# Four VectorE sums of a gate operand moved into the first gate pair, three residual sums moved behind a weight split

## The chip, the cores and the metric

The kernel runs on one core of one Trainium2 chip. The metric is the device time of one execution in microseconds, taken as the median of several runs. The kernel is written with explicit tiles; a compiler pass puts the instructions of each engine in an order and adds the semaphores. Where the code asks for it, an instruction is kept in program order on its engine; elsewhere the pass may move it.

## The reference, cut to what matters

One layer of a diffusion backbone runs on 640 tokens (512 of a sample, 128 of a prompt) with a width of 1024. Four token mixers a, b, c and d each give a 256-wide result. Each is projected to 1024 and multiplied by a sigmoid gate, and the sum goes through `w_o` and is added to the residual:

```python
g_a, g_b, g_c, g_d = split(sigmoid(h @ w_gate + b_gate), 4)        # h: 640 x 1024
merged = (g_a * (y_a @ w_br_a) + g_b * (y_b @ w_br_b)
          + g_c * (y_c @ w_br_c) + g_d * (y_d @ w_br_d))             # y_*: 640 x 256
x = x + g1 * (merged @ w_o)
h = rmsnorm(x, norm2_g) * (1 + sc2) + sh2
x = x + g2 * conv_ffn(h, w_up, ...)
```

All of it is float32. The kernel keeps that accuracy by splitting each operand into a high and a low part and adding three products: high times high, high times low, low times high. The high part is a copy on ScalarE (ACT), the low part a subtraction on VectorE (DVE), so every weight block costs one instruction on each of the two engines before TensorE (PE) can use it.

## The kernel before, in words

**Order of the stages.** Boot and adaLN; the input projection with the four mixers run beside it as generators that a planner resumes; the gates; the output projection `w_o`; the second norm; the up projection of the FFN; the down projection. TensorE is the engine that most stages are ordered around.

**Gates.** The branches come in the order d, a, b, c. Of branch d, the output blocks n = 0 and n = 4 are made singly by `gate_tile` (the product of gate and branch is written to MG by a VectorE multiply, L1014). All others are made in pairs of blocks (n, n + 4) by `g_pair`, 15 pairs, with a Winograd form of a 2 x 2 block product: seven products (`GPROD`, numbered 1 to 7) instead of eight. Products 1 to 4 take blocks of the operand as they are, products 5, 6 and 7 take differences of them. The seven products with the 1024-deep h are called `gprod` (12 matmuls each, L1187), the seven with the 256-deep branch operand `bprod` (3 matmuls each, L1196).

**Operands of h.** The generator `g_operands` (L1036 on) loads quarters of h into D, G and S0, makes the differences there (L1052), splits them into F (product 7), X1 (product 5) and X0 (product 6), and makes one more operand in D for product 3 (L1070). Once the operand of product 7 is split, its place in D is free, and `y_load(0)` puts the operand of branch d there: SP copies the high part from E, and then POOL adds the low part with an accumulating DMA (both are `D<-E`). `y_sums` makes the differences of that operand in place: four VectorE instructions of 128x320, `D<-D`. They wait for the accumulating DMA. Then the flag `gx3` is set.

**The first pair.** `g_all` waits for that flag while it is being written out, and then makes the weights of pair 0: `g_s01` (s, two sums), `g_s23` (raw, two sums), `g_b` and `g_c` (the splits into w), `g_zh` (ACT, `S<-raw`). From there on the order of VectorE, ScalarE and POOL is fixed as written, until the last pair is done. `g_pair(0)` begins with `g_zl` (DVE, `S<-raw,S`) and product 1 into b1, whose copy by ACT is `ga<-m`; `g_a` (ACT, `B<-raw`) and, in a pair that begins a branch, `y_split` (ACT, two copies `C<-D`) follow; then product 2 into b3, `g_split(3)` (ACT `XH<-D`, DVE `XL<-D,XH`), the sum of b1 and b3 (DVE `ga<-m,ga`), the sums of pair 1's weights (DVE `D<-raw,G`, `D<-D,G`), the gate's sigmoid (ACT `ga<-ga,cst`), the low parts of `y_split` (DVE `C<-D,C`), product 6 and its copy (ACT `gb<-m`), product 5, and product 7. For the branches a, b and c, `y_sums` is called at the end of the pair before the one that needs it.

**Output projection.** `wo_tile` has eight units: two halves nh of the columns by four blocks kk of the depth. For nh = 0 the four blocks are accumulated into five PSUM tiles, one for each 128 tokens (t); behind the last block each is multiplied by the gain row (DVE, L1403, `wt<-m,F`) and added to the residual (DVE, L1405, `X<-X,wt`, and `G<-G,wt` for t = 4). For nh = 1 the products wait until all four weight blocks are there. Each weight block is split by ACT (L323) and DVE (L324, `w<-raw,w`). The tiles `wt` come from a pool of four buffers. Beside this, `up_early` prepares the first weights of the up projection on the same engines (L1525, L1544, L1548), and behind each finished t of nh = 1 `norm2(t)` starts: square on ACT (L1423), a root on POOL, the scaling on DVE (L1425), and eight transposes on TensorE (L1437).

Of the kernel before, what the change touches and what calls it, by code (L numbers as in the profile page):

```python
# [13 lines left out]
ALU = mybir.AluOpType  # L14
# [56 lines left out]
def tile_step(ctx: ExitStack, tc: tile.TileContext, a: dict, outs: list, dbg=None):  # L71
# [54 lines left out]
    def nm(s):  # L126
        cnt[0] += 1
        return f"{s}_{cnt[0]}"
# [26 lines left out]
    ten, vec, pool = [Ordered(e, boot) for e in (nc.tensor, nc.vector, nc.gpsimd)]  # L155
# [882 lines left out]
    def g_operands():  # L1038
        while "cg" not in R:
            yield 1  # L1040
        d, g = region("D", [P, 2, 4, HC]), region("G", [P, 4, HC])
        yield 8
        for x, h, c in ((d[:, 0], 0, 1), (d[:, 1], 1, 1), (g, 0, 0)):
            yield 10
            nc.sync.dma_start(x, hdr[h, c])
        while "scores" not in R or "ada39" not in R:
            yield 1
        a12 = region("S0", [P, 4, HC])
        nc.sync.dma_start(a12, hdr[1, 0])
        a21, a22, a11 = d[:, 0], d[:, 1], g  # L1050
        for o, x, y in ((a22, a21, a22), (a21, a11, a21), (a11, a22, a11)):
            tc.keep_in_program_order(vec.tensor_tensor(o, x, y, ALU.subtract))  # L1052
            yield 2
        gx["x"] = {}
        for i, h, c in ((1, 0, 0), (2, 1, 0), (4, 1, 1), (3, 0, 1)):
            cs = slice(c * HC, (c + 1) * HC)
            gx["x"][i] = xh[:, 4 * h:4 * h + 4, cs], xl[h][:, :, cs]
        for i, x, t, key in ((7, a21, "F", "scores"), (5, a22, "X1", "yc"), (6, a11, "X0", "yc")):
            while key not in R:
                yield 1  # L1060
            y = region(t, [P, 2, 4, HC], F32R)
            gx["x"][i] = y[:, 0], y[:, 1]
            g_split(i, x)
            if i == 7:
                gx["Y"] = a21.rearrange("p a t -> p (a t)")
                y_load(0)
            yield 1.5
        gx["t3"] = a22, a11
        gx["S"] = a22.rearrange("p a t -> p (a t)").rearrange("p (i k c) -> p i k c", i=2, k=5)
        vec.tensor_tensor(a22, a12, a11, ALU.add)  # L1070
        y_sums()
        R["gx3"] = True

    def g_split(i, x):
# [13 lines left out]
    def y_sums():  # L1088

        a11, a21, a12, a22 = [gx["Y"][:, i * HC:(i + 1) * HC] for i in range(4)]  # L1090
        for o, x, y, f in ((a22, a21, a22, ALU.subtract), (a21, a11, a21, ALU.subtract),
                           (a11, a22, a11, ALU.subtract), (a12, a12, a11, ALU.add)):
            ovec.tensor_tensor(o, x, y, f)
# [47 lines left out]
    def g_s01(p_, r):  # L1141

        s = gw[p_, "S"] = [gx["S"][:, i] if p_ else gp.tile([P, 5, P], F32, tag="gt", name=nm("s"))
                           for i in range(2)]
        ovec.tensor_tensor(s[0], r[0][:, 0], r[1][:, 1], ALU.add)
        ovec.tensor_tensor(s[1], s[0], r[1][:, 0], ALU.add)
# [90 lines left out]
    def g_pair(p_, r):  # L1237
        n, q = p_ + 1, p_ - 1
        inner, nx = p_ < GPAIR, n < GPAIR
        if not inner:  # L1240
            g_sig(q, 1, gw[q, "gt", 1], gw[q, "gt", 1])
            g_close(q)
            g_merges(q)
            return
        bi, n0 = gp_id(p_)
        new = n0 == (NPL if bi == 0 else 0)
        if new:
            gx["bi"] = bi
        if n0 == (NPL if bi == 0 else 0) + 1 and bi < 3:
            y_load(bi + 1)  # L1250
        b1, b3 = pm()[:, 0:HC], pm()[:, 0:HC]
        ga = gw[p_, "gt", 0] = gp.tile([P, T], F32, tag="gt", name=nm("ga"))
        gb = gw[p_, "gt", 1] = gp.tile([P, T], F32, tag="gt", name=nm("gb"))
        g_zl(p_, r[p_])
        gprod(b1, p_, 1, True)
        if q >= 0:
            g_sig(q, 1, gw[q, "gt", 1], gw[q, "gt", 1])
        oact(b3 if q >= 0 else ga[:, 0:HC], b1, AF.Copy)
        if q >= 0:
            g_close(q)  # L1260
        ps = gw[p_, "ps"] = pg()
        p1_, p3_ = ps[:, 1, 0:HC], ps[:, 0, 0:HC]
        bprod(p1_, p_, 1, True)
        oact(p3_, p1_, AF.Copy)
        if q >= 0:
            g_merges(q)
        if nx:
            g_a(n, r[n])
            if q >= 0:
                g_s01(n, r[n])  # L1270
        lows, x3 = y_split() if new else ([], None)
        gprod(b3, p_, 2, q < 0)
        if q < 0:
            g_split(3, gx["t3"][0])
            ovec.tensor_tensor(ga[:, 0:HC], b3, ga[:, 0:HC], ALU.add)
            g_s01(n, r[n])
        g_sig(p_, 0, ga[:, 0:HC], b3 if q >= 0 else ga[:, 0:HC])
        for x in lows:
            low(*x)
        if nx:  # L1280
            g_al(n, r[n])
            g_s23(n, r[n])
        gprod(b1, p_, 6, False)
        oact(gb[:, 0:HC], b1, AF.Copy)
        bprod(p3_, p_, 2, False)
        b2 = pm()[:, 0:HC]
        gprod(b2, p_, 5, True)
        if nx and not new:
            g_b(n)
        gprod(b1, p_, 7, False)  # L1290
        oact(gb[:, HC:T], b1, AF.Copy)
        y = gw[p_, "y"] = gp.tile([P, T], F32, tag="gt", name=nm("y"))
        c2_ = gw[p_, "b2"] = pm()[:, 0:HC]
        bprod(p1_, p_, 6, False)
        oact(y[:, 0:HC], p1_, AF.Copy)
        bprod(c2_, p_, 5, True)
        ovec.tensor_tensor(gb[:, HC:T], b2, gb[:, HC:T], ALU.subtract)
        if new:
            g_b(n)
        if nx:  # L1300
            late = g_c(n, r[n])
            if not new:
                for x in late:
                    low(*x)
            if n + 1 < GPAIR:
                r[n + 1] = gp_load(n + 1)
        else:
            m_split(0)
            m_split(1)
        gprod(b1, p_, 4, False)  # L1310
        g_sig(p_, 0, ga[:, HC:T], b1)
        bprod(p1_, p_, 7, False)
        oact(y[:, HC:T], p1_, AF.Copy)
        if new:
            oact(x3[2], x3[1], AF.Copy)
            low(*x3)
        if nx:
            g_zh(n, r[n])
        gprod(b2, p_, 3, False)
        if n0 == (NPL if bi == 0 else 0) + 1 and bi < 3:  # L1320
            y_sums()
        ovec.tensor_tensor(y[:, HC:T], c2_, y[:, HC:T], ALU.subtract)
        ovec.tensor_tensor(gb[:, 0:HC], b2, gb[:, 0:HC], ALU.subtract)
        if new:
            for x in late:
                low(*x)
# [40 lines left out]
    hh = []  # L1367
    st2 = const.tile([P, 16], F32, name="st2")

    wo = {}  # L1370

    def wo_tile(nh, kk_, w):
        if (nh, kk_) == (0, 0):
            start(up_early(), 1)
            drain(lambda: "ada39" in R)
            grows["g1"] = gain_load(0, "F")
            xr0 = region("X0", [P, 2560])
            xr1 = region("X1", [P, 2560])
            xr2 = region("G", [P, 1280])
            x2.extend([xr0[:, 0:1024], xr0[:, 1024:2048], xr1[:, 0:1024], xr1[:, 1024:2048],  # L1380
                       xr2[:, 0:1024]])
            for t in range(5):
                pool.dma_start(x2[t], xsrc[t])
            wo["acc"] = [pm(), pm(), pg()[:, 0, :], pm(), pg()[:, 0, :]]
        wo[kk_] = w
        if nh == 1 and kk_ < 3:
            return
        for t in range(5):
            m = pm() if nh == 1 else wo["acc"][t]
            for q in (range(4) if nh == 1 else (kk_,)):  # L1390
                for k in (2 * q, 2 * q + 1):
                    for i, (hx, hw) in enumerate(((0, 0), (0, 1), (1, 0))):
                        mm(m, mh[MHN[q]][:, hx, k % 2, t * P:(t + 1) * P], wo[q][:, hw, k % 2, :],  # L1393
                           start=(k == 0 and i == 0), stop=(k == 7 and i == 2))
                    tick(0.65)
            if (nh, kk_, t) == (0, 3, 4):
                R["half"] = True
            if kk_ < 3:
                continue
            v = 0 if t < 4 else 1  # L1400
            tmp = gp.tile([P, 512], F32, tag="gt", name=nm("wt"))
            cs = slice(nh * 512, nh * 512 + 512)
            vec.tensor_tensor(tmp, m, grows["g1"][:, v, cs], ALU.mult)  # L1403
            xs = x2[t][:, cs]
            vec.tensor_tensor(xs, xs, tmp, ALU.add)  # L1405
            if nh == 1:
                start(norm2(t))
                tick(0)
# [52 lines left out]
    for nh in range(2):  # L1461
        for kk_ in range(4):
            plain(lambda nh=nh, kk_=kk_: rows(a["w_o"][nh, MHN[kk_]], 2, 512,
                                              "MG0" if (nh, kk_) == (1, 0) else None),
                  lambda w, nh=nh, kk_=kk_: wo_tile(nh, kk_, w))
# [1099 lines left out]
```

## Time and profile before

| what | value |
|---|---|
| median of 3 runs (lowest, highest) | 1006.76 us (1006.0, 1009.12) |
| the profiled execution's own time | 1006.04 us |
| its span, first to last instruction | 1004.2 us |
| mean granted TensorE clock | 0.995 |
| busy: PE / DVE / ACT / POOL | 98% / 87% / 58% / 17% |
| chain that ended last: PE / DVE / DMA | 88% / 5% / 4% |

The busy shares are means over stages with different limits. A busy PE in these views is modelled, since matmuls are pipelined; what counts for it is where it had to wait and for whom. Names left of `<-` are what an instruction writes, those on the right what it reads; `L151` is the line of the helper through which the ordered instructions go, so in the gates an instruction is known by its tiles.

### The profile page before, as it was taken

How to read it: one execution, taken by the hardware profiler on the slowest of the kernel's cores; microseconds unless marked ns; L12 is line 12 of the kernel's file. 1: busy time of each engine (PE TensorE's matmuls, PEld its weight loads, DVE VectorE, ACT ScalarE, POOL GpSimd, SP SyncE). 2: the span in 40 equal slices, each digit the busy share in tenths (PEclk: the TensorE clock that was granted, in tenths of full speed). 3: DMA queues.
4: the chain of work that ended last, by engine and by line, in shares of the span. 5: the costliest groups of instructions: out<-in, count | busy, mean ns of one | idle time of the engine just before them, and what ended most of it. 6: DMA issues, size and time to landing. Idle time of an engine off the chain costs nothing.

```text
span 1004.2 us, 18954 instructions
## 1 busy us (share of the span) xinstructions
PE 987.3 (98%) x7452; PEld 935.0 (93%) x7452; DVE 869.5 (87%) x1425; ACT 587.2 (58%) x1018; POOL 168.3 (17%) x225
## 2 busy tenths in 40 slices
PE   8999999999989999999999999999999999999997
PEld 6899999999989999999998799999999999888886
DVE  6678899878769889898878978999999998999796
ACT  6642343445446555655656377777777777756672
POOL 1000020322111223241000021222222222100004
PEclk9999999999999999999999999999999999999999
DMA  9875344498465799899248875766666666976842
GB/s 353 334 252 163 111 149 124 125 258 252 120 215 179 275 230 287 248 276 235 85 132 331 321 284 181 219 159 174 173 163 169 177 169 194 353 259 226 292 127 105
DMA packets 70730, 212.86 MB, mean 212 GB/s; under 512 B 9713, under 2 KB 24849, under 8 KB 67953
## 3 DMA queue, kind: packets, MB, share of 16 engines
q1 hardware_dynamic: 43968, 151.22, 43.0%
q0 software_dynamic: 26672, 60.43, 26.3%
q8 instruction: 58, 0.95, 0.4%
q14 instruction: 32, 0.25, 0.1%
HBM read 168.62 MB, written 48.51 MB: 216 GB/s over the span
## 4 chain that ended last, share of the span: by engine, by line
PE 88%; DVE 5%; DMA 4%; issue 1%; POOL 1%; ACT 1%; SPq 0%; POOLq 0%; DVEq 0%; ACTq 0%
PE g L1623 21%; PE m L1187 18%; PE g L375 12%; PE m L2095 9%; PE m L1623 5%; PE g L2095 4%; PE g L1196 3%; PE g L948 2%; PE m L1393 2%; PE m L151 2%; PE g L151 1%; PE m L1196 1%; DMA D<-E 1%; PE m L539 1%; PE m L1618 1%
## 5 line engine op out<-in xcount | busy, mean ns | idle before, releaser
L375 PE MATMUL g<-XH,w 128*128 128x320 f32 x640 | 155.0, 317 | 0.0
L375 PEld LDWEIGHTS g<-XH,w 128*128 128x128 f32 x640 | 109.5, 188 | 2.5 <-issue 1.2
L375 PE MATMUL g<-XL,w 128*128 128x320 f32 x320 | 98.8, 309 | 0.0
L1187 PE MATMUL m<-XH,w 128*128 128x320 f32 x368 | 87.4, 309 | 0.0
L1187 PEld LDWEIGHTS m<-XH,w 128*128 128x128 f32 x368 | 63.2, 188 | 0.2 <-ACT gb L151 0.2
L375 PEld LDWEIGHTS g<-XL,w 128*128 128x128 f32 x320 | 60.3, 188 | 0.0
L2095 PE MATMUL m<-w,XH 128*128 128x512 f32 x246 | 58.6, 390 | 0.0
L1187 PE MATMUL m<-XL,w 128*128 128x320 f32 x184 | 56.9, 309 | 0.0
L2095 PEld LDWEIGHTS m<-w,XH 128*128 128x128 f32 x246 | 46.1, 188 | 9.5
L151 ACT ACTIVATE w<-raw 128x640 fp32r<-128x640 f32 (+3 forms) x54 | 49.8, 938 | 3.4 <-DMA raw<-in_w_in_dram 2.0
L1187 PE MATMUL m<-X,w 128*128 128x320 f32 x264 | 45.2, 320 | 3.7 <-ACT ga L151 3.7
L151 DVE TENSOR_TENSOR w<-raw,w 128x640 fp32r<-128x640 f32 (+3 forms) x46 | 46.9, 1037 | 0.9 <-ACT w L151 0.8
L1187 PEld LDWEIGHTS m<-X,w 128*128 128x128 f32 x264 | 41.8, 197 | 4.0 <-ACT ga L151 4.0
L151 POOL DMA_DIRECT2D wsum<-in_w_dn_dram x36 | 37.8, 1407 | 32.1 <-issue 26.4
L151 DVE SCALAR_TENSOR_TENSOR X<-MG,p2t,X 128x641 f32<-128x641 f32 x44 | 38.9, 883 | 1.0 <-ACT X L151 0.2
L151 DVE SCALAR_TENSOR_TENSOR X<-X,p2t,X 128x641 f32<-128x641 f32 x44 | 38.9, 883 | 0.9
L1623 PE MATMUL g<-XL,w 128*128 128x320 f32 x240 | 38.6, 310 | 0.0
L151 ACT ACTIVATE gb<-m 128x320 f32<-128x320 f32 x30 | 13.1, 437 | 43.5 <-PE m L1187 43.5
L1623 PE MATMUL g<-XL,C 128*128 128x320 f32 x240 | 38.3, 309 | 0.0
L1623 PEld LDWEIGHTS g<-XL,w 128*128 128x128 f32 x240 | 36.0, 188 | 0.6 <-ACT MG L151 0.3
L1623 PEld LDWEIGHTS g<-XL,C 128*128 128x128 f32 x240 | 35.9, 188 | 0.0
L1187 PEld LDWEIGHTS m<-XL,w 128*128 128x128 f32 x184 | 34.5, 188 | 0.0
(614 smaller groups left out, 2869.4 us busy)
## 6 DMA issues: line engine op xcount, KB each, us to landing
wsum<-in_w_dn_dram POOLq DMA_DIRECT2D x30, 512.0 KB, 11.9
raw<-in_w_up_dram SPq DMA_DIRECT2D x30, 512.0 KB, 5.2
raw<-in_w_gp_dram SPq DMA_DIRECT2D x23, 640.0 KB, 6.6
raw<-in_w_in_dram SPq DMA_DIRECT2D x19, 512.0 KB, 4.3
H<-in_w_adt_dram SPq DMA_DIRECT2D x19, 512.0 KB, 3.8
raw<-wsum SPq DMA_DIRECT2D x12, 512.0 KB, 5.8
actx<-X POOLq DMA_DIRECT2D x22, 256.0 KB, 5.0
wsum<-wsum POOLq DMA_DIRECT2D x10, 512.0 KB, 12.6
```

What stands on the lines that cost most here:

```text
L151: r = f(*args, **kw)
L375: mm(o, w[:, h, k0 + k, :], r(k)[:, s], start=(k == 0 and i == 0), stop=(k == kt - 1 and i == 2))
L539: mm(m[W * g:W * g + W, (i - s0) * W:(i - s0 + 1) * W], lhs, rhs, start=True, stop=True, tile_position=(64 * par, W * g))
L948: mm(o, x(kx)[:, ts], w[:, h, k, :], start=(kx == 0 and i == 0), stop=(kx == 7 and i == 2))
L1187: mm(o, w[:, h, n, k, :], x[:, k, :], start=(first and k == 0 and j == 0), stop=(k == 3 and j == 2), skip_group_check=True)
L1196: mm(o, w[:, h, n, 4, :], x[l], start=(first and j == 0), stop=(j == 2), skip_group_check=True)
L1393: mm(m, mh[MHN[q]][:, hx, k % 2, t * P:(t + 1) * P], wo[q][:, hw, k % 2, :], start=(k == 0 and i == 0), stop=(k == 7 and i == 2))
L1618: mm(o, w[:, k, :], x[:, k, :], start=(first and not part and k == 0 and j == 0), stop=(part == 1 and k == 3), skip_group_check=True)
L1623: z = mm(o, w[:, k, :], x[:, k, :], start=(first and k == 0 and j == 0), stop=(k == 3 and j == 2), skip_group_check=True)
L2095: mm(ps, s[t // 4][:, hx, k, o:o + P], w[:, hw, k, c0:c1], start=first, stop=i == 2 and bi == len(batch) - 1 and k == len(ks) - 1, skip_gr ...
```

## The change

`y_sums` for branch d is no longer called in `g_operands` before the flag is set, but in `g_pair(0)` behind `g_a` and ahead of `y_split`. There the order of VectorE is fixed, so the four sums stand behind `g_zl` and ahead of `XL<-D,XH`, and all the weight work of pair 0 that `g_all` writes is no longer behind them in the program. In `wo_tile`, the residual sums of nh = 0 for t = 2, 3 and 4 are not issued with their products but kept in a list, and issued when the last weight block of nh = 1 is taken up, ahead of its first product.

```diff
@@ g_operands
         vec.tensor_tensor(a22, a12, a11, ALU.add)
-        y_sums()
         R["gx3"] = True
@@ g_pair
             g_a(n, r[n])
             if q >= 0:
                 g_s01(n, r[n])
+        if q < 0:
+            y_sums()
         lows, x3 = y_split() if new else ([], None)
         gprod(b3, p_, 2, q < 0)
@@ wo_tile
-    wo = {}
+    wo = {"late": []}
...
         if nh == 1 and kk_ < 3:
             return
+        if nh == 1:
+            for xs, tmp in wo["late"]:
+                vec.tensor_tensor(xs, xs, tmp, ALU.add)
         for t in range(5):
...
             vec.tensor_tensor(tmp, m, grows["g1"][:, v, cs], ALU.mult)
             xs = x2[t][:, cs]
+            if nh == 0 and t > 1:
+                wo["late"].append((xs, tmp))
+                continue
             vec.tensor_tensor(xs, xs, tmp, ALU.add)
```

## The prediction

> **What bounds the kernel now.** I read the page's chain of waits first.
>
> ```profile
> PE 88%; DVE 5%; DMA 4%; issue 1%; POOL 1%; ACT 1%; SPq 0%; POOLq 0%; DVEq 0%; ACTq 0%
> ```
>
> TensorE carries the chain, so an edit on VectorE pays only where TensorE waits. Next I asked for whom TensorE waited around the two edited places (260 to 330 us, and 518 to 600 us); each answer has one row: engine, what waits, for what, total us, times, longest.
>
> ```profile
> PE m L1187 <- ACT ga L151: 3.7, 1, 3.7
> PE m L1393 <- DVE w L324: 1.4, 1, 1.4
> ```
>
> Each edit sits at one of TensorE's waits: 3.7 us in the first gate pair, 1.4 us in the output projection. The VectorE timeline (start, us, engine, line, operation, idle time before) shows where the first comes from.
>
> ```profile
> 284.15 1.48 DVE L151 TENSOR_TENSOR X<-G,X 128x1280 fp32r<-128x1280 f32 x1
> 293.14 1.54 DVE L151 TENSOR_TENSOR D<-D 128x320 f32<-128x320 f32 x3 [7.51 <-DMA D<-E]
> 294.61 0.82 DVE L151 TENSOR_TENSOR s<-raw,raw 128x640 f32<-128x640 f32 x1
> ...
> 296.48 0.82 DVE L1014 TENSOR_TENSOR MG<-g,gt 128x640 f32<-128x640 f32 x1
> 297.21 0.81 DVE L151 TENSOR_TENSOR raw<-raw 128x640 f32<-128x640 f32 x1
> 297.94 0.82 DVE L151 TENSOR_TENSOR raw<-s,raw 128x640 f32<-128x640 f32 x1
> 298.68 1.55 DVE L151 TENSOR_TENSOR w<-s,w 128x640 fp32r<-128x640 f32 x2
> ...
> 301.62 0.82 DVE L151 TENSOR_TENSOR S<-raw,S 128x640 fp32r<-128x640 f32 x1
> 303.43 1.49 DVE L151 TENSOR_TENSOR XL<-D,XH 128x1280 fp32r<-128x1280 f32 x1 [0.99 <-ACT XH L151]
> ...
> 306.83 1.22 DVE L151 TENSOR_TENSOR C<-D,C 128x640 fp32r<-128x640 f32 x2
> ```
>
> VectorE idles 7.51 us until the DMA for `y_sums` lands. The two s sums do not need that DMA, yet they run only behind three of the four `D<-D`, and from 293.14 to 302.44 VectorE works without a gap. ScalarE and TensorE hang on that row of work:
>
> ```profile
> 298.06 0.74 ACT L151 ACTIVATE S<-raw 128x640 fp32r<-128x640 f32 x1 [0.61 <-DVE raw L151]
> 298.70 0.42 ACT L151 ACTIVATE ga<-m 128x320 f32<-128x320 f32 x1
> ...
> 301.16 1.08 ACT L151 ACTIVATE C<-D 128x640 fp32r<-128x640 f32 x2
> 302.15 1.25 ACT L151 ACTIVATE XH<-D 128x1280 fp32r<-128x1280 f32 x1
> 305.36 0.57 ACT L151 ACTIVATE ga<-ga,cst 128x320 f32<-128x320 f32 x1 [1.96 <-DVE ga L151]
> 305.83 0.42 ACT L151 ACTIVATE gb<-m 128x320 f32<-128x320 f32 x1
> ```
>
> ```profile
> 290.77 0.75 PE L375 MATMUL g<-E,w 128*128 128x320 f32 x4
> 295.17 0.31 PE L1187 MATMUL m<-XH,w 128*128 128x320 f32 x1
> 299.17 0.90 PE L1187 MATMUL m<-X,w 128*128 128x320 f32 x2 [3.69 <-ACT ga L151]
> 306.93 1.92 PE L1187 MATMUL m<-F,S 128*128 128x320 f32 x12
> 308.69 0.46 PE L1196 MATMUL g<-C,w 128*128 128x320 f32 x2
> ```
>
> TensorE ends its first two products at 295.48 and waits for `ga<-m`, which stands in ScalarE's queue behind `S<-raw`, which waits for VectorE's raw sum, which was behind the sums. The windows add a second price, in the column PEclk (the sixth value after the window, ahead of the DMA share):
>
> ```profile
> 294.70:298.10 3.40, 0.78 (x6) 0.52 (x4) 3.40 (x6) 2.03 (x4) 0.00 (x0) 1.00 1.03 417
> 298.10:301.50 3.40, 2.28 (x7) 1.88 (x8) 3.40 (x5) 3.40 (x6) 0.00 (x0) 0.50 0.15 60
> 301.50:304.90 3.40, 3.40 (x15) 3.40 (x14) 2.41 (x4) 1.90 (x3) 0.00 (x0) 0.50 0.73 227
> 559.50:562.90 3.40, 1.97 (x9) 1.31 (x9) 3.40 (x6) 0.63 (x1) 0.00 (x0) 1.00 0.72 269
> ```
>
> After a window with 0.78 of 3.40 us busy, the granted clock is 0.50 for 6.8 us. The idle 1.4 us near 562 (1.97 of 3.40 busy) left it at 1.00.
>
> **Part one, the four sums.** At full clock twelve matmuls `m<-F,S` take 1.76 us (306.93 to 308.69), 0.147 each. Between 299.17 and 306.93 TensorE issues 33 matmuls (first and last rows above), 4.85 us at that rate; without any wait it would come to `m<-F,S` at 295.48 + 4.85 = 300.33 instead of 306.93. So 6.6 us is the most that this place can give.
>
> What really binds is the row behind the sums. Product 7 (`m<-F,S`) needs `gb<-m`, which ended at 306.25 behind the sigmoid, the sum `ga`, `XL<-D`, `XH<-D`, `C<-D`. TensorE came 0.68 us after it. So TensorE gains as much as the start of `XL<-D` gains, plus about 0.6, up to 6.6. After the change `C<-D` still needs `y_sums`, now written behind `S<-raw,S`, so VectorE's work up to there has to be laid out anew.
>
> VectorE is free at 284.15 + 1.48 = 285.63. The work before `y_sums` is s, s, raw, raw, four low parts w, S, and `MG`, the second single gate's product, which needs TensorE's `g<-E` ending at 290.77 + 0.75 = 291.52. Steps are 0.73 to 0.74 (297.21, 297.94, 298.68); the four low parts 2.94 (298.68 to 301.62). Where the compiler puts `MG` decides, and the trace of before does not show it:
>
> - `MG` right behind the s sums, as now: VectorE waits from 287.1 to 291.56, then 0.73 (MG) + 1.47 (raw) + 2.94 (w) + 0.73 (S): `y_sums` at 297.4.
> - `MG` behind the raw sums too: these are done at 288.6; from 291.56, 0.73 + 2.94 + 0.73: `y_sums` at 296.0.
> - `MG` behind the low parts: all is done by about 293, and `y_sums` starts as the DMA lands, 293.14.
>
> I take the middle one: now 3.34 us of VectorE's work stand ahead of `MG` from 293.14 on; without the sums the compiler has s, s, raw, raw (2.94 us) to put there.
>
> The price of four chained sums is read where the same routine runs inside pair 1, one row; that sum stands beside no other:
>
> ```profile
> 326.79 2.06 DVE L151 TENSOR_TENSOR D<-D 128x320 f32<-128x320 f32 x4
> ```
>
> So `y_sums` ends at 298.0, the two `C<-D` at 299.0 (0.99, from 301.16 to 302.15), `XH<-D` at 300.3 (1.25), and `XL<-D` starts at 300.3 instead of 303.43: 3.1 us earlier. TensorE starts `m<-F,S` at about 303.2 instead of 306.93, a gain of **3.7 us**, after an idle 2.9 us (300.33 to 303.2). The low parts `C<-D,C`, ending 306.83 + 1.22 = 308.05 now, come at 304.95, as product 7 ends (304.96). The other two cases give 2.3 us (`XL<-D` at 301.7) and the full 6.6 us. From 309 to 526 us TensorE has no idle, and what follows starts from its end:
>
> ```profile
> 309.00:526.00 217.00, 217.00 (x1480) 216.79 (x1480) 188.56 (x256) 128.81 (x211) 47.36 (x54) 1.00 0.83 218
> ```
>
> VectorE has 28 us to spare there, so the gain passes through whole. No DMA is moved: the SP copy, POOL's accumulating DMA and the weight sums behind it on POOL keep their places in their queues, and the sums themselves issue none. `XH<-D` and all behind it on ScalarE now wait for `y_sums` too; that is in the 3.1 us.
>
> **Part two, the three residual sums.**
>
> ```profile
> 560.03 0.67 DVE L1405 TENSOR_TENSOR X<-X,wt 128x512 f32<-128x512 f32 x1
> 560.63 0.67 DVE L1405 TENSOR_TENSOR G<-G,wt 128x512 f32<-128x512 f32 x1
> 561.23 1.21 DVE L324 TENSOR_TENSOR w<-raw,w 128x1024 fp32r<-128x1024 f32 x1
> 560.00:570.00 10.00, 8.57 (x38) 6.79 (x37) 10.00 (x16) 3.69 (x5) 0.00 (x0) 1.00 0.77 290
> 571.94 0.75 DVE L1425 TENSOR_SCALAR C<-X,st 128x1024 f32<-128x1024 f32 x1 [0.47 <-POOL st L318]
> 572.75 1.09 PE L1437 MATMUL m<-cst,C 128*128 128x128 f32 x8
> ```
>
> Three sums at 0.60 each stand ahead of the last low part. With them behind it, it starts up to 1.8 us earlier and ends by 560.65; TensorE, whose wait of 1.4 us ended with the low part at 562.44, wanted it at about 561.0, and need not wait: 1.4 us there. What is late next is the first transposes: they start at 572.75, right as `C<-X` ends at 572.69. `C<-X` closes a row of VectorE work that has the same instructions in it before and after, since the three sums are only moved inside it. If TensorE comes there 1.4 us earlier with the same order, it waits 1.4 us there. I take **0**, with 1.4 us as the upper end (the compiler puts the transposes a group of matmuls later); a loss is excluded because VectorE is full (10.00 of 10 us from 560 to 570, the third value) with the same work either way. Three `wt` buffers of four are held longer; the fourth is enough for the next product.
>
> **The sum.** 3.7 + 0 from the profiled 1006.04 gives 1002.3. That execution lies 0.7 under the median and level with the lowest run, so I set the undisturbed time at 1006.4 and predict **1002.7**.
>
> **Rivals.**
> 1. *Nothing left to wait for* (`MG` late): 6.6 us, perhaps 1.4 more from part two: 999.8, at best 998.4. For it: VectorE's 7.5 us of idle would hold all of its 7.4 us of work ahead of `y_sums` (0.73 each for two s, `MG`, two raw and S, 2.94 for the low parts). Against it: `MG` cannot start before 291.56.
> 2. *The clock drops again.* My middle case leaves TensorE idle for 2.9 us. A window 77% idle cost half speed for 6.8 us, one 42% idle cost nothing. If 2.9 us suffice, half speed for one window of 3.4 us loses 1.7, for two 3.4: 1004.4 to 1006.1. The Trainium skill, "TensorE: Matmul & The Clock Gate", Part 1, says the clock halves after an idle window of about 3.4 us on a free-running grid and returns after a busy one. By that rule 2.9 us of idle never fill a window, and my sum would stand; the trace speaks against its letter, since it dropped with 0.78 us of work in the window.
> 3. *Slower*: `MG` stays right behind the s sums, and TensorE idles from 300.33 to 304.6, 4.3 us, longer than the 3.69 that dropped the clock. Then half speed for 6.8 us loses 3.4 with VectorE ahead, while now part of that loss hides behind VectorE. 2.3 - 3.4 = -1.1: 1007.5. It decides once the idle passes about 3.7 us and TensorE gets no full window of work before the second one.
> 4. *The compiler keeps its order* in part two because the sums are ready earlier than the low part: 0, as in my sum.
>
> **Chances.** Middle case 0.34 (1001.3 to 1003.3, with part two between), rival 1 0.24, rival 2 or the first layout without a drop (1004.1) 0.34, rival 3 0.08. A measurement here can tell about 0.3%, 3.0 us, from no change. The middle case lies past that bound mostly, so faster gets 0.56, same 0.36, slower 0.08. The range reaches from rival 1 to the drop that eats the gain: 999.2 to 1006.4.
>
> **What would show it.** `s<-raw,raw` starting near 285.6, with VectorE's wait now before `MG` (for PE) and none for `D<-E`; four `D<-D` in one row behind `S<-raw,S`, near 296; `ga<-m` on ScalarE near 293.2; no wait of TensorE at 295.5 and a shorter one before `m<-F,S`; PEclk 1.00 from 290 to 310. In the output projection: L324 ahead of `G<-G,wt`, no wait for it, and instead one for `C` before L1437. I am wrong if the compiler orders `MG` otherwise, if PEclk still drops, or if the pairs behind 309 show new idle time.

## The result, and the profile after

The changed kernel takes 1004.59 us (median of 20 runs, 1003.07 to 1007.0). The kernel before, run beside it on the same chip, takes 1006.21 us (20 runs, 1005.32 to 1009.12). The ratio is 0.9982, with a 95% interval of 0.9975 to 0.9989: 1.8 us less (1.1 to 2.5), where 3.7 were forecast. The profiled execution took 1004.91 us, its span is 1003.1 us. Behind `y_sums` the line numbers stand one lower (L1187 is L1186); from the output projection on they stand up to seven higher.

TensorE's waits from 260 to 330 us come first: engine, what waits, for what, total us, times, longest.

```profile
PE m L1186 <- DVE ga L151: 2.6, 1, 2.6
PE m L1186 <- ACT gb L151: 0.4, 1, 0.4
```

The wait of 3.7 us for the copy `ga<-m` is gone. In its place 2.6 us stand further back, ahead of the last two matmuls in front of product 7 (`m<-XH,B` and `m<-XL,B`), and 0.4 us ahead of product 7 itself.

VectorE's timeline of the changed kernel (start, us, engine, line, operation, idle time before):

```profile
287.04 0.82 DVE L151 TENSOR_TENSOR raw<-raw 128x640 f32<-128x640 f32 x1
291.52 0.82 DVE L1014 TENSOR_TENSOR MG<-g,gt 128x640 f32<-128x640 f32 x1 [3.67 <-PE g L375]
292.27 0.81 DVE L151 TENSOR_TENSOR raw<-s,raw 128x640 f32<-128x640 f32 x1
...
295.94 0.82 DVE L151 TENSOR_TENSOR S<-raw,S 128x640 fp32r<-128x640 f32 x1
296.68 2.06 DVE L151 TENSOR_TENSOR D<-D 128x320 f32<-128x320 f32 x4
300.54 1.49 DVE L151 TENSOR_TENSOR XL<-D,XH 128x1280 fp32r<-128x1280 f32 x1 [1.80 <-ACT XH L151]
```

ScalarE and TensorE at the same place:

```profile
289.69 0.80 ACT L1003 ACTIVATE gt<-g,cst 128x640 f32<-128x640 f32 x1 [6.23 <-PE g L375]
290.39 1.35 ACT L151 ACTIVATE w<-s 128x640 fp32r<-128x640 f32 x2
293.27 0.44 ACT L151 ACTIVATE ga<-m 128x320 f32<-128x320 f32 x1 [0.28 <-PE m L1186]
298.24 1.10 ACT L151 ACTIVATE C<-D 128x640 fp32r<-128x640 f32 x2 [2.39 <-DVE D L151]
```

```profile
303.40 2.75 PE L1186 MATMUL m<-F,S 128*128 128x320 f32 x12 [0.36 <-ACT gb L151]
309.15 0.60 PE L1195 MATMUL g<-C,S 128*128 128x320 f32 x3
```

`MG` stands behind one raw sum. The four `D<-D` follow `S<-raw,S`, `XL<-D` starts at 300.54 instead of 303.43, and product 7 at 303.40 instead of 306.93: 3.53 us earlier. Then the twelve matmuls take 2.75 us, where 1.92 is what the group took before, and the windows say why (PEclk is the sixth value after the window):

```profile
304.00:305.00 1.00, 1.00 (x7) 1.00 (x6) 1.00 (x3) 0.00 (x0) 0.00 (x0) 0.70 0.02 8
305.00:306.00 1.00, 1.00 (x6) 1.00 (x5) 1.00 (x2) 0.00 (x0) 0.00 (x0) 0.50 0.00 0
307.00:308.00 1.00, 1.00 (x6) 1.00 (x6) 1.00 (x3) 1.00 (x2) 0.00 (x0) 0.59 0.00 0
308.00:309.00 1.00, 1.00 (x8) 1.00 (x8) 1.00 (x3) 1.00 (x3) 0.00 (x0) 1.00 0.00 0
```

From 304.4 to 307.8 the granted clock is 0.50. The row `g<-C,S` at 309.15 stood at 311.25 before, so 2.1 of the 3.53 us are left. The row of before:

```profile
311.25 0.60 PE L1196 MATMUL g<-C,S 128*128 128x320 f32 x3
```

In the output projection the low part L324 has two of the three sums behind it (the first still stands ahead), and TensorE's wait is now the transposes' (L1444), for `C<-X`:

```profile
557.57 1.22 DVE L324 TENSOR_TENSOR w<-raw,w 128x1024 fp32r<-128x1024 f32 x1
...
569.50 0.75 DVE L1432 TENSOR_SCALAR C<-X,st 128x1024 f32<-128x1024 f32 x1 [0.47 <-POOL st L318]
```

```profile
570.31 1.09 PE L1444 MATMUL m<-cst,C 128*128 128x128 f32 x8 [1.18 <-DVE C L1432]
```

The wait for L324 (1.4 us) is gone, one of 1.18 us has taken its place, and the transposes start 2.44 us earlier than before (572.75). Another 1.15 us are lost at the start of the down projection, where ScalarE waits for a load, in a place where the trace of before has no wait. The load's row before and after (issue to landing in us, at the end), then the timeline after:

```profile
C<-actp SPq DMA_DIRECT2D x1, 704.0 KB, 4.2
C<-actp SPq DMA_DIRECT2D x1, 704.0 KB, 5.8
```

```profile
858.09 0.42 ACT L1999 ACTIVATE MG<-C 128x256 fp32r<-128x256 f32 x1 [1.45 <-DMA C<-actp]
...
859.58 2.00 PE L1630 MATMUL g<-XL,w 128*128 128x320 f32 x12 [1.15 <-DVE X L151]
```

The load of 704 KB landed 5.8 us after its issue, against 4.2 us in the profile of before, where nobody waited for it. So the two profiled spans differ by 1.1 us, less than the medians do.

### The profile page after: what moved, and what is told of

It is laid out like the page before. It is cut to its first block, busy times and chain, and to the rows that moved or that the text cites. A ratio compares the mean times of both kernels' runs of the same rounds, so it can differ in the third digit from the quotient of the medians.

```text
span 1003.1 us, 18956 instructions
## 1 busy us (share of the span) xinstructions
PE 987.3 (98%) x7452; PEld 935.3 (93%) x7452; DVE 870.0 (87%) x1425; ACT 587.3 (59%) x1018; POOL 168.2 (17%) x225
## 4 chain that ended last, share of the span: by engine, by line
PE 87%; DVE 5%; DMA 3%; issue 2%; ACT 1%; POOL 1%; SPq 0%; POOLq 0%; DVEq 0%; ACTq 0%
PE g L1630 20%; PE m L1186 18%; PE g L375 14%; PE m L2102 9%; PE m L1630 5%; PE g L2102 4%; PE g L1195 3%; PE g L948 2%; PE m L151 2%; PE g L151 1%; PE m L1397 1%; PE m L1195 1%; PE m L539 1%; PE m L1625 1%; DMA A<-in_w_ada_dram 1%
## 5 line engine op out<-in xcount | busy, mean ns | idle before, releaser
L1186 PE MATMUL m<-XH,w 128*128 128x320 f32 x368 | 87.6, 310 | 0.0
L1186 PEld LDWEIGHTS m<-XH,w 128*128 128x128 f32 x368 | 63.5, 189 | 0.0
L1186 PE MATMUL m<-XL,w 128*128 128x320 f32 x184 | 57.0, 310 | 0.0
L1186 PE MATMUL m<-X,w 128*128 128x320 f32 x264 | 42.8, 309 | 0.0
L1186 PEld LDWEIGHTS m<-X,w 128*128 128x128 f32 x264 | 39.7, 188 | 0.0
L1186 PEld LDWEIGHTS m<-XL,w 128*128 128x128 f32 x184 | 34.7, 189 | 0.0
```

The source lines that it names most:

```text
L1186: mm(o, w[:, h, n, k, :], x[:, k, :], start=(first and k == 0 and j == 0), stop=(k == 3 and j == 2), skip_group_check=True)
```

## The experiments

**Part one alone.** The three residual sums stay in their place.

```diff
-    wo = {"late": []}
+    wo = {}
...
-        if nh == 1:
-            for xs, tmp in wo["late"]:
-                vec.tensor_tensor(xs, xs, tmp, ALU.add)
...
-            if nh == 0 and t > 1:
-                wo["late"].append((xs, tmp))
-                continue
```

> Only the four sums are moved; the three residual sums stay where they were. My theory: the first gate pair alone carries the gain. Against the kernel before -1.6 to -2.2 us, so 1004.0 to 1004.6. In the profile: VectorE waits for PE ahead of MG (3.7 us), TensorE waits 2.6 us for DVE ga and 0.4 for ACT gb, the granted clock is 0.50 for about one window of 3.4 us afterwards, and the 1.4 us wait for the last low part (L324) is still there, with no wait before the first transposes. Rival: the gain of the first pair is lost in the clock drop and the residual sums bring the 1.6 us; then this kernel takes 1005.9 to 1006.5.

Measured: 1004.74 us (12 runs) against 1006.81; ratio 0.9977 (0.9967 to 0.9986), that is 2.3 us less (1.4 to 3.3), the change's gain within the intervals; the median lies 0.14 us above the range expected. TensorE's waits in the output projection (518 to 600 us), and the window behind the gate's idle time:

```profile
PE m L1394 <- DVE w L324: 1.6, 1, 1.6
PE m L1438 <- DVE C L1426: 0.3, 1, 0.3
```

```profile
300.00:310.00 10.00, 7.08 (x45) 6.36 (x44) 9.10 (x11) 5.20 (x9) 0.00 (x0) 1.00 0.22 87
```

```profile
303.73 2.02 PE L1186 MATMUL m<-F,S 128*128 128x320 f32 x12 [0.36 <-ACT gb L151]
...
308.14 0.60 PE L1195 MATMUL g<-C,S 128*128 128x320 f32 x3
```

The idle time is the same 2.56 + 0.36 us, but the clock stays at 1.00 against the expectation, and `g<-C,S` comes at 308.14. The 0.3 us at the transposes were not expected either. Part one carries the gain, and the same idle time has two prices.

**Part two alone.** `y_sums` goes back to its place.

```diff
         vec.tensor_tensor(a22, a12, a11, ALU.add)
+        y_sums()
...
-        if q < 0:
-            y_sums()
         lows, x3 = y_split() if new else ([], None)
```

> Only the three residual sums are moved; the four sums stay in the generator. My theory: the wait for the last low part (1.4 us) is gone and TensorE waits 1.2 to 1.4 us instead for DVE C before the first transposes, so 0 to -0.3 us: 1005.9 to 1006.2. The first gate pair as before, with the 3.7 us wait for ACT ga and half clock for 6.8 us. Rival (the residual sums bring the gain): 1004.5 to 1004.9, and no new wait before the transposes.

Measured: 1006.56 us (12 runs) against 1006.81; ratio 0.9997 (0.9988 to 1.0006). TensorE's waits from 260 to 330 us, and from 518 to 600:

```profile
PE m L1187 <- ACT ga L151: 3.7, 1, 3.7
...
PE m L1443 <- DVE C L1431: 1.2, 1, 1.2
PE m L1396 <- DVE w L324: 0.7, 1, 0.7
```

The gate's wait is back, here with half clock for one window of 3.4 us and not for 6.8. Of the wait for L324 0.7 us stay in this execution, where none were expected, and 1.2 stand at the transposes: 1.9 against 1.4 before. The wait for L324 is not gone in the other executions with the late sums either: 0.2 to 0.6 us of it are left in all but the first profile of the changed kernel. The part is worth nothing that can be measured.

**The gate ahead of the sums.** To the changed kernel: `XH`/`XL`, the sum and the sigmoid of `ga` and the copy `gb` are written ahead of `y_sums` and the copies `C<-D`.

```diff
         if q < 0:
-            y_sums()
-        lows, x3 = y_split() if new else ([], None)
+            g_split(3, gx["t3"][0])
+        lows, x3 = y_split() if new and q >= 0 else ([], None)
         gprod(b3, p_, 2, q < 0)
         if q < 0:
-            g_split(3, gx["t3"][0])
             ovec.tensor_tensor(ga[:, 0:HC], b3, ga[:, 0:HC], ALU.add)
-            g_s01(n, r[n])
         g_sig(p_, 0, ga[:, 0:HC], b3 if q >= 0 else ga[:, 0:HC])
+        if q < 0:
+            gprod(b1, p_, 6, False)
+            oact(gb[:, 0:HC], b1, AF.Copy)
+            y_sums()
+            lows, x3 = y_split()
+            g_s01(n, r[n])
...
-        gprod(b1, p_, 6, False)
-        oact(gb[:, 0:HC], b1, AF.Copy)
+        if q >= 0:
+            gprod(b1, p_, 6, False)
+            oact(gb[:, 0:HC], b1, AF.Copy)
```

> The changed kernel, with XH/XL, the sum ga, the sigmoid and the copy gb of pair 0 written ahead of the four sums and the C copies. My theory: what binds is the row y_sums, C, XH, XL, ga, sigmoid, gb; taken out of it, product 7 starts without a wait near 299.9, the next wait is for the low parts C (about 303.6, so up to 2 us), and the clock stays at 1.00 or nearly. 2.2 to 3.2 us less than the changed kernel: 1001.4 to 1002.4. Rival: VectorE's amount of work ahead of product 7 and the C parts binds, whatever its order, or the accumulating DMA does; then TensorE's wait only moves to the C parts with its full length, the clock drops again, and it takes 1004.2 to 1004.9.

Measured: 1002.08 us (5 runs, 1001.57 to 1002.96); ratio 0.9953 (0.9941 to 0.9965), 4.7 us less than before. VectorE, then TensorE:

```profile
297.76 1.49 DVE L151 TENSOR_TENSOR XL<-D,XH 128x1280 fp32r<-128x1280 f32 x1 [0.29 <-ACT XH L151]
...
299.57 2.06 DVE L151 TENSOR_TENSOR D<-D 128x320 f32<-128x320 f32 x4
```

```profile
300.63 2.03 PE L1186 MATMUL m<-F,S 128*128 128x320 f32 x12 [0.28 <-ACT gb L151]
```

`XL<-D` no longer waits for the sums, and product 7 starts at 300.63 after 0.28 us of idle time, and the clock stays at 1.00. So the 2.6 us were the four sums, the copies `C<-D` and the split, in VectorE's and ScalarE's queues ahead of `XL<-D`. About 1 us of the wait only moved: TensorE now waits 0.67 us for the last low part (tile `y`) and 0.36 us for a copy, 10 us further on.

**The gate's sigmoid later.** To the changed kernel: the second single gate's sigmoid (`gt`) and its product (`MG`) are written behind pair 0's weight work.

```diff
-        act(c2(gt), ps[:, :, 0:HC], AF.Sigmoid, bias=p1[:, gc:gc + 1])
+        last = (bi, n) == (0, 4)
+        if not last:
+            act(c2(gt), ps[:, :, 0:HC], AF.Sigmoid, bias=p1[:, gc:gc + 1])
...
-        if bi == 0:
+        if last:
+            def rest():
+                act(c2(gt), ps[:, :, 0:HC], AF.Sigmoid, bias=p1[:, gc:gc + 1])
+                vec.tensor_tensor(c2(mg), pbv, c2(gt), ALU.mult)
+            gx["rest"] = rest
+        elif bi == 0:
...
         g_zh(0, r[0])
+        gx["rest"]()
```

> The changed kernel, with the sigmoid and the multiply MG of the second single gate written behind the weight work of pair 0, so that VectorE and ScalarE do not stand waiting for TensorE's branch product at 291.5 with that work behind them. My theory: y_sums start at about 294.4 instead of 296.7, and TensorE starts product 7 about 2.3 us earlier, after less than 1 us of idle, with the clock at 1.00. 3 to 4 us less than the changed kernel: 1000.6 to 1001.6. Rival: the place of MG does not matter because the DMA (landing at 293.1) or ScalarE's queue holds the sums; then within 0.5 us of the changed kernel.

Measured: 1002.11 us (5 runs, 1001.12 to 1002.37); ratio 0.9949 (0.9937 to 0.9961), 5.1 us less than before by the ratio and 4.7 by the medians; the median is 0.5 us above the range expected. VectorE, then TensorE:

```profile
291.91 0.82 DVE L1018 TENSOR_TENSOR MG<-g,gt 128x640 f32<-128x640 f32 x1 [1.45 <-PE g L375]
...
294.86 2.06 DVE L151 TENSOR_TENSOR D<-D 128x320 f32<-128x320 f32 x4
```

```profile
301.59 2.02 PE L1193 MATMUL m<-F,S 128*128 128x320 f32 x12 [0.36 <-ACT gb L151]
```

With the sigmoid out of the way VectorE has done one raw sum and two low parts more by the time it reaches `MG`, and the sums start at 294.86 instead of 296.68. The rival, by which nothing would change, did not come. This is another way to the same 1002 us. Both runs take the idle time and the drop of the clock away together; what each costs apart is read from the executions that follow.

**The kernel before, and the changed one, once more.** One execution each, to see what varies from one execution to the next.

> The kernel before, profiled once more, to see what differs between two executions of the same kernel. My theory of the 1.1 us that the changed kernel loses at the start of the down projection: the load C<-actp takes 4.0 to 5.9 us from one execution to the next and TensorE waits as soon as it takes over 4.3, whatever the gates did; then this execution may well show a wait of 0.5 to 1.2 us there. Rival: the changed order brought it; then none here, and the load takes about 4.2. In the gate pair: the same 3.7 us wait, with half clock for 3.4 or 6.8 us, by where the idle falls on the clock's windows.

> The changed kernel, profiled once more. The waits of the first pair as in its first profile (2.6 for DVE ga, 0.4 for ACT gb): the order is the same. My theory of the clock: whether this idle halves it depends on where it falls on windows of 3.4 us, so this execution may show it at 1.00 throughout; if it drops, then for 3.4 or 6.8 us. Rival: the idle decides alone; then the clock drops again for 3.4 us, at the same place.

The kernel before took 1007.77 us this time. ScalarE and TensorE at the start of the down projection:

```profile
860.97 0.42 ACT L1992 ACTIVATE MG<-C 128x256 fp32r<-128x256 f32 x1 [1.78 <-DMA C<-actp]
...
862.46 2.00 PE L1623 MATMUL g<-XL,w 128*128 128x320 f32 x12 [1.47 <-DVE X L151]
```

The load that nobody waited for in the first profile of before landed after 6.2 us here, and TensorE lost 1.47 us. So the wait occurs without the change too. In the ten profiled executions the load took 4.0 to 6.2 us and TensorE waited 0 to 1.5 us: 0 at 4.0 and 4.2, 0.2 to 0.3 at 4.9 and 5.0, 0.7 to 0.8 at 5.4 and 5.5, 1.1 to 1.5 from 5.8 on. Long and short landings occur with and without part one: the mean wait is 0.75 us in the three executions with the old gate code and 0.70 us in the seven others. So nothing here points to the change as its cause.

The gate pair has the same wait of 3.7 us, but half clock for one window instead of two. The window, the copy `gb<-m` and product 7 of this second execution:

```profile
299.65:303.06 3.41, 3.02 (x12) 2.96 (x12) 2.77 (x4) 3.41 (x6) 0.00 (x0) 0.50 0.25 62
305.81 0.42 ACT L151 ACTIVATE gb<-m 128x320 f32<-128x320 f32 x1
306.28 2.03 PE L1187 MATMUL m<-F,S 128*128 128x320 f32 x12
```

The copy stands within 0.02 us of where it stood in the first execution (305.83), but product 7 starts right behind it, 0.65 us earlier than the 306.93 of there. In the first execution TensorE was held up by the second window of half clock, and came late.

The changed kernel took 1006.56 us. Its windows, and the row behind them:

```profile
304.00:305.00 1.00, 1.00 (x5) 1.00 (x5) 1.00 (x3) 0.00 (x0) 0.00 (x0) 0.50 0.03 8
...
308.00:309.00 1.00, 1.00 (x5) 1.00 (x5) 0.55 (x2) 1.00 (x2) 0.00 (x0) 0.50 0.00 0
```

```profile
310.27 0.60 PE L1195 MATMUL g<-C,S 128*128 128x320 f32 x3
```

Behind the same 2.56 us of idle time (the 0.4 for `gb` are not there) the clock is now at half speed from 302.4 (worked out in the last section) to 309.2, two windows. So the idle time alone does not decide, which was the rival. From the start of product 7 to `g<-C,S` it is 4.41 us in the execution without a drop (303.73 to 308.14), 5.75 with one window (303.40 to 309.15), 6.75 with two (303.52 to 310.27). A drop thus costs 1.3 or 2.3 us of what the change gains by then. By the first matmul of the output projection 0.3 of it is won back: that matmul comes 222.4 us behind the start of product 7 in both executions without a drop, 223.4 with one window, 224.4 with two.

**The first norm ahead of the early sums.** A try at the 1.2 us at the transposes: the second half of the up projection's early VectorE work (`up_early`) is resumed only once the first `norm2` has started.

```diff
-            while p_ and "half" not in R:
+            while p_ and "t0" not in R:
                 yield 0.5
...
                 start(norm2(t))
                 tick(0)
+                if t == 0:
+                    R["t0"] = True
...
         fx["x"] = {1: (hh[0][:, 0], hh[0][:, 1]), 2: (hh[0][:, 2], hh[0][:, 3])}
+        drain(lambda: "early" in R)
         up_back(2, "A", unit(2, 0), 0, 4)
```

> The changed kernel, with the second half of up_early (XH and XL sums and splits of the up weights) resumed only after the first norm2 has been started, so that wt, X and C<-X of t = 0 stand ahead of it on VectorE. My theory: the residual sums' 1.4 us were given back at the first transposes because C<-X is late; with C<-X about 3 us earlier there is no wait before the transposes, and it takes 1.0 to 1.4 us less than the changed kernel: 1003.2 to 1003.7. Rival: the wait only moves on, to the weights of the up projection that up_early now prepares later, or to the next transposes; then within 0.4 us of the changed kernel.

Measured: 1005.21 us (11 runs) against 1006.41; ratio 0.9987 (0.9978 to 0.9996), not told apart from the changed kernel and short of what was hoped for, as the rival had it. TensorE:

```profile
568.65 1.03 PE L1446 MATMUL m<-cst,C 128*128 128x128 f32 x8
...
575.64 0.66 PE L1446 MATMUL m<-cst,C 128*128 128x128 f32 x4 [1.34 <-DVE C L1434]
```

The first transposes no longer wait, but the second tile's do, for 1.34 us: VectorE's work is only put off. In this execution, too, the clock stayed at 1.00 behind the gate's idle time.

**All three edits together.** The edits of the last three kernels on top of the change.

> The changed kernel with all three edits: gate row of pair 0 ahead of the four sums, MG behind pair 0's weights, and norm2 ahead of up_early's second half. My theory: the two gate edits overlap, since each alone leaves under 1.5 us of idle in the first pair, so together they give 0.5 to 1.2 us more than one; with the 1.2 us of the transposes 1.5 to 2.4 us less than either gate edit alone: 999.7 to 1000.6. Rival: VectorE's total work in the first pair is the floor, so the gate edits give nothing together and only the 1.2 us of the transposes come: 1000.9.

Measured: 1001.78 us (5 runs, 1001.45 to 1002.21); ratio 0.9953 (0.9939 to 0.9966). This is the lowest median, but not told apart from either gate edit alone, and above both the range expected and the rival's 1000.9. Both gate edits take away the same wait, so they don't add up: the output projection's first matmul starts at 525.01 and 523.99 with one of them and at 523.95 with both. The second tile's transposes wait for 1.32 us, as in the run with the norm's edit alone.

## Why the prediction was right in its mechanism and too high in its gain

- **The layout of VectorE's work**: `MG` came behind one raw sum, not two, so the sums start at 296.68 instead of 296.0. Their price was 2.06 us, as read from pair 1. ScalarE starts the copies `C<-D` at 298.24, before the last sum is done, which wins back most of the 0.7 us: `XL<-D` at 300.54 against 300.3, product 7 at 303.40 against 303.2, a gain of 3.53 us against 3.7. The idle time is 2.92 us against 2.9.
- **"Plus about 0.6" is a term that belonged to one execution.** The prediction read that TensorE came 0.68 us behind `gb<-m`, and counted that as gain. In the second execution of before, with one window of half clock, product 7 came right behind the copy, at 306.28, and with part two alone TensorE waited 0.30 us for it. So the 0.6 was a second window of half clock in the profile from which the sum was made. Against 306.28 the gain at product 7 is 2.88 us.
- **Rival 1 (the full 6.6 us)** was rightly held off, for half of the reason. The prediction saw only `MG` on VectorE. ScalarE's queue was blocked as well: ScalarE stands idle for 6.23 us ahead of the sigmoid `gt`, which waits for TensorE's `g` until 289.69, and the weight highs `w<-s` behind it come at 290.39, so VectorE's low parts could not have run in the idle time whatever the place of `MG`. The run with both moved gave sums at 294.86, not at the DMA's 293.14.
- **PEclk 1.00 is the step that failed.** The middle case, on which the sum stands, took the 2.9 us of idle time as harmless. In the four profiled executions with this gate code the clock stayed up twice, dropped for one window once, and for two windows once. So rival 2 is what came, in half of them: it priced one window at 1.7 us and the time at 1004.4; a window cost 1.3 us at the end of the pair, 1.0 of which are left at the output projection, and the median is 1004.59. That the two times lie so close is partly luck, as 1004.4 also holds the 0.6 us too much of gain. The measured time lies in the stated range, 999.2 to 1006.4, which was wide enough for rivals 1 and 2, and outside the middle case's 1001.3 to 1003.3. The Trainium skill, "TensorE: Matmul & The Clock Gate", Part 1, was weighed in rival 2: by its idle window of about 3.4 us no drop was due. These traces go against that part: the clock dropped twice behind 2.56 us of idle time.
- **"The gain passes through whole"** holds to 0.4 us from 309 to 526 us: from `g<-C,S` to the first matmul of the output projection it is 217.7 to 218.0 us in all seven executions with the old gate code or this one. It missed that the time at the end also carries the landing of `C<-actp`, with a wait of 0 to 1.5 us with and without part one. The profiled execution of before from which the sum was made was one without that wait; the second one had it and ran 1.7 us longer. The starting point does not explain the miss, though: the 1006.4 that was set lies above the 1006.21 measured. The gain was too large.
- **The sum with what was measured.** 2.9 us at product 7, less the mean cost of the drop in the four executions, (0 + 0 + 1.0 + 2.0) / 4 = 0.75, is an estimate of 2.1 us, where 1.8 (1.1 to 2.5) were measured. Four executions are few for such a mean.
- **Part two at 0** was right, by its own reason: 1.4 us at L324 became 1.2 us at the transposes, as `C<-X` closes a row of VectorE work that did not get shorter. Rival 4 was wrong, since the order did change. Rival 3 (slower) did not come, as `MG` was not right behind the s sums.

The timed runs fit this, but do not show it. The changed kernel's 20 runs spread over 3.9 us, with mean granted clocks from 0.992 to 0.998. The 15 runs of the three kernels whose gate idle time is short, five each, spread over 1.4, 1.3 and 0.8 us, with 0.997 to 0.999. Fewer runs spread less in any case, the load's landing adds its part, and a mean clock covers the whole execution, so that the drop in the gates can't be told from others.

## What to carry to other kernels

When a wait of the bottleneck engine is cut down but not removed, ask whether what is left can still lower its clock, and price that as a term of the sum with the spread that it brings. Before counting on an engine's idle time, look at what stands at the head of the other engines' queues in that stretch: one sigmoid waiting for a matmul kept the work from filling it. A second profiled execution of the kernel before shows which waits, and which lags, belong to one execution only: here 0.6 us of the forecast gain.

## What was not expected of the hardware

In these traces the clock's steps lie on a fixed grid, and a window need not be empty to lower it. The first two rows are the changed kernel's, the last two those of its second execution: half a microsecond around the first drop, and around the drop behind the last matmul.

```profile
304.00:304.50 0.50, 0.50 (x5) 0.50 (x4) 0.50 (x2) 0.00 (x0) 0.00 (x0) 0.91 0.05 16
1000.50:1001.00 0.50, 0.00 (x0) 0.00 (x0) 0.00 (x0) 0.00 (x0) 0.00 (x0) 0.73 1.07 434
```

```profile
302.00:302.50 0.50, 0.00 (x0) 0.00 (x0) 0.50 (x3) 0.00 (x0) 0.00 (x0) 0.86 0.08 31
1002.00:1002.50 0.50, 0.00 (x0) 0.00 (x0) 0.00 (x0) 0.00 (x0) 0.00 (x0) 0.59 1.12 451
```

A mean of 0.91 over 0.5 us means half speed from 304.41 on (0.82 of the half microsecond at full speed); the others give 1000.73, 302.36 and 1002.09. The distances are 696.32 and 699.73 us: they differ by one window, 3.41 us, and are 204 and 205 times 3.4133. That agrees with the free-running window of 3413 ns that the Trainium skill, "TensorE: Matmul & The Clock Gate", Part 1, states. The grid's place against the kernel differs between executions.

Set on that grid, the last window ahead of the changed kernel's drop, and the emptiest window in the gates of the run with part one alone, where the clock did not drop:

```profile
301.00:304.41 3.41, 1.57 (x9) 1.31 (x10) 3.38 (x5) 0.89 (x2) 0.00 (x0) 1.00 0.25 100
```

```profile
298.72:302.13 3.41, 1.53 (x11) 1.26 (x9) 1.61 (x2) 2.11 (x3) 0.00 (x0) 1.00 0.97 384
```

TensorE was busy for 1.57 us in the first and for 1.53 in the second. The drop of before had 0.78. Busier windows lie on both sides as well: with all three edits the clock dropped, behind the last matmul, after a window with 1.82 us, and in the second execution of before it stayed up after one with 1.77:

```profile
991.53:994.95 3.42, 1.82 (x17) 1.65 (x15) 2.52 (x10) 1.28 (x3) 0.60 (x2) 1.00 0.15 59
```

```profile
559.06:562.47 3.41, 1.77 (x8) 1.13 (x6) 3.41 (x5) 0.62 (x1) 0.00 (x0) 1.00 0.89 328
```

Estimated from these, the bound lies between about 1.5 and 1.8 us of modelled work per window, where either can happen. So about 2.6 us of idle time drop the clock or don't, by where the grid falls. When it comes back is not settled: it came back after a window with 3.02 us (299.65 to 303.06 in the second execution of before) and not after one with 3.15 (302.36 to 305.77 in that of the changed kernel). Busy times are modelled, and no bound on them sorts the windows seen.
